# Attention decays of a hybrid GLA layer: prefix sums over tokens by a VectorE scan instead of 0/1 matrices on TensorE

## The chip, the cores and the metric

The kernel runs on one core of one Trainium2 chip. The metric is the device time of one execution in microseconds. The core's engines work beside each other, each through its own instruction queue in order: TensorE (PE; its weight loads are PEld), VectorE (DVE), ScalarE (ACT), GpSimd (POOL), and SyncE (SP), which here only issues DMA transfers. An instruction that waits for a semaphore holds everything behind it on its engine.

## The reference

One layer over 256 latent tokens (2048 channels) with 256 context tokens: a token mixer (gated linear attention beside a pooling mixer, merged by gates) and a SwiGLU feed-forward part. The change touches only the decays of the attention. Cut to that:

```python
q, k, v, g, a_lr, p, bg = jnp.split(proj, SPLIT_POINTS, axis=-1)
for d in range(2):                       # two directions
    z = a_lr[..., d*16:(d+1)*16] @ w_decay_up[d] + b_decay_up[d]
    log_decay.append(_heads(jax.nn.log_sigmoid(z) / 16.0, HEAD_K))

# per head, chunks of 64 tokens
cum = jnp.cumsum(log_a, axis=3)          # running sum over the tokens of a chunk
ref = cum[:, :, :, 31:32]
q_in, k_in = q * jnp.exp(cum - ref), k * jnp.exp(ref - cum)
scores = where(lower_triangle, q_in @ k_in.T, 0)
last = cum[:, :, :, -1:]
q_inter, k_state = q * jnp.exp(cum), k * jnp.exp(last - cum)
decay_chunk = jnp.exp(last)              # carries the state from chunk to chunk
```

There are 4 heads with 256 key channels and 512 value channels each. The context is scanned first, and its final state is where the latent tokens start.

The modulation, `silu(c) @ w_ada + b_ada`, yields six vectors of 2048 channels per condition. Only those for the first sub-layer's input are needed early; the others are needed behind the attention.

## The kernel before

All matrix products run on fp32 operands split into a high and a low part (fp32r). Weights arrive as units of 128x1024 numbers (512 KB): SP issues the transfer into a buffer `raw`, ScalarE writes `hi` (L100), VectorE subtracts to get `lo` (L101), and TensorE multiplies. `ws_tile` (L130, L134) has the weight stationary and yields channels by tokens; `nat_block` (L160, L161, L163) has the activations stationary and yields tokens by channels. The three buffers of each kind and eight PSUM banks set how far ahead this can run. A scheduler with priorities and a cost model sets each engine's order when the kernel is built; the splits have a raised priority.

The stages in time: modulation of the input and projection v (0 to 236 us), projection k for latent and context tokens with the low-rank decay rows `alr` (`kT_half`, 236 to 334), projection q of heads 0 and 1 (`qT_half(0)`, 334 to 356), the attention (356 to 606), which includes `front(0)`, the gate projection `g_block(0)`, `qT_half(1)`, and a loop over the heads of `back(h)`, `front(h+1)` and `g_block(h+1)`, then the pooling projection; then gates and merging (610 to 930), output projection and norm (to 1060), feed-forward in (to 1540) and out (to 1792).

`front(h)` makes, for each of two directions d, all decay factors of a head, multiplies q and k by them, and forms the masked score matrices PT (latent) and PC (context). `log_sigmoid` (L461 on) multiplies `alr` by the decay weights `wd` to get z with tokens on the partitions, and splits the log decay into `la` high and low. Sums over tokens are then matrix products with `cm`, a constant of 0/1 matrices (L507 for the context, L521 for the latent tokens), whose results ScalarE exponentiates straight from PSUM (L510, L522, L523) and VectorE multiplies by q or k (L511, L533 to L542). The score matmuls are L550, L553, L558 and L564. `back(h)` applies them to v.

The rest of the modulation is filler: `ada(n)` takes the next n units of `w_adaT`, for each of which SP moves 512 KB into a buffer `ra` and VectorE does one multiply with a sum (L269). `ADA` says how many are taken where: 4 per tile of projection k, 1 per tile of projection q, 8 per head, and 2 per step (16 steps, `ct`) of the gates stage, with what is left in its last steps. `ra` has three buffers during projection k and `qT_half(0)`, one in the attention, and two in the gates stage.

Of the kernel before, what the change touches and what calls it, by code (L numbers as in the profile page):

```python
# [41 lines left out]
ADA = (0, 1, 4, 2, 8, 8)  # L42
# [14 lines left out]
C_LAT = (0, 512)  # L57
C_CTX = 1024
C_N = 1664


@with_exitstack
def trunk(ctx, tc, small, consts, masks, xT, ctxT, x_nat, lnrows, wdec, pmat, c_row,
# [162 lines left out]
    with ExitStack() as c1:  # L226
# [156 lines left out]
        pk = c1.enter_context(sub_pool("pk"))  # L383
        cQ = ExitStack()
# [30 lines left out]
        def kT_half(b):  # L415
# [43 lines left out]
        def log_sigmoid(h, d, base, wd, ztmp):  # L459

            la = pg.tile([P, U], F32R, tag="la", bufs=2, name=nm("la")).rearrange("p (s t d) -> p s t d", s=2, t=2)  # L461
            z = bank("g")
            for t in range(2):
                PE.matmul(z[:, t * HK:(t + 1) * HK], alr[:, base + t * P:base + (t + 1) * P], wd[:, d, :],
                          start=(t == 0), stop=True, skip_group_check=True)
            e = ztmp
            S.activation(e, z, AF.Abs)
            S.activation(e, e, AF.Exp, scale=-1.0)
            S.activation(e, e, AF.Ln, bias=1.0)
            V.scalar_tensor_tensor(e, z, 0.0, e, op0=ALU.min, op1=ALU.subtract)  # L470
            split(e.rearrange("p (t d) -> p t d", t=2), la[:, 0], la[:, 1])
            return la

# [7 lines left out]
        def front(h):  # L481
            hb, ho = divmod(h, 2)
            wr = pg.tile([P, 2, HK], F32, tag="tmp", bufs=2, name=nm("wr"))
            nc.gpsimd.dma_start(wr, wdec[:, :, h * HK:(h + 1) * HK])
            wd = pg.tile([P, 2, HK], F32R, tag="wd", bufs=1, name=nm("wd"))
# [3 lines left out]
            kTh = kT[hb][:, 2 * ho:2 * ho + 2, :]  # L489
            qTh = qT[hb][:, 2 * ho:2 * ho + 2, :]  # L490
            kch = kTc[hb][:, 2 * ho:2 * ho + 2, :]
            PT = pg.tile([P, 4, P], F32, tag="PT", bufs=NPT, name=nm("PT"))
            PC = pg.tile([P, 2, T], F32, tag="PC", bufs=NPT, name=nm("PC"))
            for d in range(2):
                bun = hcp.tile([P, 4096], F32, tag="hc", name=nm("bun"))
                E = bun[:, :2304].rearrange("p (c n) -> p c n", c=2)
                kst = bun[:, 2304:2816].rearrange("p (c j) -> p c j", c=2)
                q4 = bun[:, 2816:3328].rearrange("p (c t i) -> p c t i", c=2, t=2)
                zt = bun[:, 3328:3840]

                la = log_sigmoid(h, d, T, wd, zt)
                ex = bank("g")
                for c in range(2):
                    for t in range(2):
                        b = C_CTX + 256 * d + 128 * (1 - t)
                        for s in range(2):
                            PE.matmul(ex[:, c * T:(c + 1) * T], la[:, s, t, c * P:(c + 1) * P], cm[:, b:b + T],  # L507
                                      start=(c == 0 and t == 0 and s == 0), stop=(t == 1 and s == 1),
                                      skip_group_check=True)
                S.activation(kst, ex.rearrange("p (c j) -> p c j", c=2), AF.Exp, scale=1.0 / 16.0)  # L510
                V.tensor_tensor(kst, kst, kch, op=ALU.mult)  # L511

# [562 lines left out]
```

## Time and profile before

| what | us |
|---|---|
| median of 3 runs | 1794.83 (1792.32 to 1798.92) |
| the profiled execution, its own time | 1794.45 |
| its span, first to last instruction | 1792.5 |
| TensorE busy in it | 1753.0 |
| mean granted clock of TensorE | 0.993 of full speed |

The profile is of one execution. A matmul's listed length runs past the start of the next one, since matmuls are pipelined; what one costs is the distance from its start to the start of the next. The same holds, to a lesser degree, for VectorE. A wait is listed at the engine that stood idle, with the instruction that ended it. Line numbers are those of the kernel before; in the changed kernel the same helpers stand five lines higher (L101 is L96 there, L130 is L125, L160 is L155, L269 is L264).

### The profile page before, as it was taken

To read this page: it belongs to the slowest core of one execution; us is meant where nothing else is said; L and a number is where in the kernel's file an instruction comes from. 1 tells how busy PE (TensorE), PEld (TensorE's weight loads), DVE (VectorE), ACT (ScalarE), POOL (GpSimd) and SP (SyncE) were. 2 spreads that over 40 slices of the span, in tenths; PEclk is the share of its full clock that TensorE was granted. 3 is DMA by queue.
4 is the path that set the end of the run, shared out by engine and by line. 5 is a ranking of instruction groups with operands and counts; after the bars stand their busy time and mean duration, and the time that the engine had idled before them with its cause. 6 is when DMAs were issued, how large, how long until landed. Compare 5 with 4: busy or idle time off the path is not lost.

```text
span 1792.5 us, 24735 instructions
## 1 busy us (share of the span) xinstructions
PE 1753.0 (98%) x9549; PEld 1468.0 (82%) x9551; DVE 1165.6 (65%) x1725; ACT 801.7 (45%) x1179; POOL 8.0 (0%) x17
## 2 busy tenths in 40 slices
PE   8999999999999999999999989999999999999996
PEld 5667878877777788888887878888888888888886
DVE  3665466576898576776666766666666666554555
ACT  2212222374776454444444464445444444443432
POOL 0000000000000000000000000000000000000000
PEclk9999999999999999999999999999999999999998
DMA  9895258755566467777786635577777766556553
GB/s 385 295 358 183 83 201 283 244 171 176 171 206 211 165 221 248 236 236 257 236 288 219 210 118 189 188 246 259 246 236 247 237 233 234 188 191 196 191 189 126
DMA packets 109350, 394.16 MB, mean 220 GB/s; under 512 B 12176, under 2 KB 12304, under 8 KB 108720
## 3 DMA queue, kind: packets, MB, share of 16 engines
q1 hardware_dynamic: 107712, 385.10, 63.0%
q0 software_dynamic: 1520, 7.47, 1.1%
q8 instruction: 75, 1.23, 0.3%
q14 instruction: 43, 0.35, 0.1%
HBM read 390.43 MB, written 2.10 MB: 219 GB/s over the span
## 4 chain that ended last, share of the span: by engine, by line
PE 75%; DVE 5%; DMA 3%; ACT 2%; issue 1%; SPq 0%; ACTq 0%; DVEq 0%
PE ps L130 33%; PE ps L134 17%; PE ps L160 6%; PE ps L161 6%; PE ps L163 6%; DMA raw<-in_w_o 1%; DVE lo L101 1%; ACT hi L100 1%; PE ps L564 1%; DMA ra<-in_w_adaT 1%; PE ps L592 1%; DVE ra L269 1%; PE ps L550 1%; PE ps L521 0%; PE ps L407 0%
## 5 line engine op out<-in xcount | busy, mean ns | idle before, releaser
L101 DVE TENSOR_TENSOR lo<-raw,hi 128x1024 fp32r<-128x1024 f32 x510 | 623.3, 1224 | 462.6 <-ACT hi L100 446.7
L100 ACT ACTIVATE hi<-raw 128x1024 fp32r<-128x1024 f32 x510 | 539.9, 1060 | 689.6 <-PE ps L130 263.8
L130 PE MATMUL ps<-h,hi 128*128 128x512 f32 x1408 | 353.4, 392 | 0.8 <-DVE h L101 0.8
L130 PEld LDWEIGHTS ps<-h,hi 128*128 128x128 f32 x1408 | 253.3, 189 | 46.5 <-DVE h L101 1.2
L130 PE MATMUL ps<-hl,hi 128*128 128x512 f32 x768 | 211.9, 393 | 0.0
L134 PEld LDWEIGHTS ps<-h,lo 128*128 128x128 f32 x1408 | 192.5, 190 | 13.9
L134 PE MATMUL ps<-h,lo 128*128 128x256 f32 x1408 | 196.8, 282 | 0.0
L130 PEld LDWEIGHTS ps<-hl,hi 128*128 128x128 f32 x768 | 139.8, 189 | 25.3
L160 PE MATMUL ps<-hi,hid 128*128 128x512 f32 (+1 forms) x372 | 134.9, 369 | 0.0
L161 PE MATMUL ps<-hi,hid 128*128 128x512 f32 (+1 forms) x372 | 134.0, 369 | 0.0
L160 PE MATMUL ps<-hi,hl 128*128 128x512 f32 x320 | 128.0, 400 | 2.0 <-ACT hi L100 2.0
L161 PE MATMUL ps<-hi,hl 128*128 128x512 f32 x320 | 125.6, 393 | 0.0
L134 PE MATMUL ps<-hl,lo 128*128 128x256 f32 x768 | 120.7, 282 | 0.0
L269 DVE SCALAR_TENSOR_TENSOR ra<-ra,silb 128x1024 f32<-128x1024 f32 x96 | 114.9, 1221 | 8.6 <-DMA ra<-in_w_adaT 7.9
L134 PEld LDWEIGHTS ps<-hl,lo 128*128 128x128 f32 x768 | 111.8, 190 | 6.8
L163 PE MATMUL ps<-lo,hl 128*128 128x512 f32 x320 | 92.7, 391 | 0.0
L163 PE MATMUL ps<-lo,hid 128*128 128x512 f32 x372 | 90.6, 369 | 0.0
L347 DVE TENSOR_TENSOR v<-ps,v 128x512 f32<-128x512 f32 x80 | 50.5, 684 | 55.6 <-PE ps L163 55.5
L160 PEld LDWEIGHTS ps<-hi,hid 128*128 128x128 f32 x372 | 69.8, 188 | 12.2 <-DVE xt L776 0.2
L161 PEld LDWEIGHTS ps<-hi,hid 128*128 128x128 f32 x372 | 70.0, 188 | 11.8
L160 PEld LDWEIGHTS ps<-hi,hl 128*128 128x128 f32 x320 | 60.0, 188 | 21.6 <-issue 5.2
L163 PEld LDWEIGHTS ps<-lo,hid 128*128 128x128 f32 x372 | 66.2, 188 | 11.8
(250 smaller groups left out, 2096.6 us busy)
## 6 DMA issues: line engine op xcount, KB each, us to landing
raw<-in_w_fi SPq DMA_DIRECT2D x176, 512.0 KB, 4.2
ra<-in_w_adaT SPq DMA_DIRECT2D x96, 512.0 KB, 4.6
raw<-in_w_fo SPq DMA_DIRECT2D x88, 512.0 KB, 4.3
rw<-in_w_sh_sc SPq DMA_DIRECT2D x64, 512.0 KB, 7.1
raw<-in_w_bg SPq DMA_DIRECT2D x64, 512.0 KB, 4.3
raw<-in_w_v SPq DMA_DIRECT2D x32, 512.0 KB, 5.1
raw<-in_w_g SPq DMA_DIRECT2D x32, 512.0 KB, 3.9
raw<-in_w_go SPq DMA_DIRECT2D x32, 512.0 KB, 3.4
```

Source lines behind the costliest of these rows:

```text
L100: S.activation(hi, full, AF.Copy)
L101: last_split[:] = [V.tensor_tensor(lo, full, hi.bitcast(F32), op=ALU.subtract)]
L130: PE.matmul(o, hi[:, j * P:(j + 1) * P], act(n + j), start=(n + j == 0), stop=(n + j == nk - 1), skip_group_check=True)
L134: PE.matmul(o[:, :T], lo[:, j * P:(j + 1) * P], act(n + j)[:, :T], start=False, stop=(n + j == nk - 1), skip_group_check=True)
L160: PE.matmul(o, ah, hi[:, a:b], start=(n + j == k0), stop=False)
L161: PE.matmul(o, al, hi[:, a:b], start=False, stop=False)
L163: PE.matmul(o, ah, lo[:, a:b], start=False, stop=(n + j == end))
L269: V.scalar_tensor_tensor(r, r, 1.0, silb[half], op0=ALU.mult, op1=ALU.mult, accum_out=mods[:, half, i:i + 1])
L347: V.tensor_tensor(dst, src, dst, op=ALU.add)
L550: PE.matmul(sc[:, t * P:(t + 1) * P], E[:, c, b + (512 if b == 0 else 384):b + (640 if b == 0 else 512)], E[:, c, b:b + 128], start=first, ...
L564: PE.matmul(scc[:, t * T:(t + 1) * T], kst[:, c, t * P:(t + 1) * P], q4[:, c].rearrange("p t i -> p (t i)"), start=(c == 0 and t == 0), st ...
L592: PE.matmul(os[t], PC[:, j, t * P:(t + 1) * P], vc[h][:, j, :], start=(j == 0), stop=False)
```

## The change

The 0/1 matrices, `log_sigmoid` with its split, and the products L507 and L521 go. z is now made with `wd` stationary, 128 channels by all 512 tokens (context and latent) per matmul, 4 per head (two channel halves by two directions). For each direction one `tensor_tensor_scan` on VectorE over 128 partitions by 1024 (two channel halves by 512 tokens) yields the running sums; a mask that is 0 at the segments' starts resets them. Sums over other ranges come by subtraction (VectorE), then ScalarE's exponentials run from SBUF to SBUF, then VectorE multiplies by k, and behind a `yield` by q.

`decay_up(h)`, which loads and prepares `wd`, is apart from `front` and has a pool of its own. `front(0)` is started before `qT_half(0)` and its two steps stand around it, so that the pool of projection k with its three `ra` buffers is closed before `qT_half(0)`. ADA becomes 2 per tile of q, 4 per tile of k but for the first, 3 per step of the gates stage, and 2 per head.

```diff
-ADA = (0, 1, 4, 2, 8, 8)
+ADA = (0, 2, 4, 3, 8, 2)
...
                 if b == 0 and i == 0:
                     decay_rows()
-                ada(ADA[2])
+                else:
+                    ada(ADA[2])
...
+        def front(h, wd):
...
             for d in range(2):
...
+                x = xs[d]
                 for c in range(2):
...
+                    z = bank("g")
+                    PE.matmul(z, wd[:, d, c * P:(c + 1) * P], alr, start=True, stop=True)
+                    e = x[:, d + 512 * c:d + 512 * c + 512]
+                    S.activation(e, z, AF.Abs)
+                    S.activation(e, e, AF.Exp, scale=-1.0)
+                    S.activation(e, e, AF.Ln, bias=1.0)
+                    V.scalar_tensor_tensor(e, z, 0.0, e, op0=ALU.min, op1=ALU.subtract)
...
+                if d == 0:
+                    V.tensor_tensor_scan(Wf, mask, x[:, 0:1024], 0.0, op0=ALU.mult, op1=ALU.add)
+                else:
+                    V.tensor_tensor_scan(Wf, x[:, 0:1024], mask, 0.0, op0=ALU.add, op1=ALU.mult)
...
+                V.tensor_tensor(G.rearrange("p c (n i) -> p c n i", n=4), W64,
+                                W64[:, :, :, 31 + d:32 + d].to_broadcast([P, 2, 4, 64]), op=ALU.subtract)
+                V.tensor_tensor(TT.rearrange("p c t n i -> p c t (n i)"), Wl,
+                                Wl[:, :, :, 63 + d:64 + d].to_broadcast([P, 2, 2, P]), op=ALU.subtract)
...
+                S.activation(ep, G, AF.Exp, scale=sc16)
+                S.activation(G, G, AF.Exp, scale=-sc16)
...
+                V.tensor_tensor(k1, k1, kh, op=ALU.mult)
+                V.tensor_tensor(TT[:, :, :, d, :], TT[:, :, :, d, :], kv[:, :, :, d, :], op=ALU.mult)
+                V.tensor_tensor(k3, k3, kh[:, :, f * P:(f + 1) * P], op=ALU.mult)
+                V.tensor_tensor(kst, kst, kch, op=ALU.mult)
+                yield
...
+                V.tensor_tensor(q1, q1, qh, op=ALU.mult)
...
-        qT_half(0)
         cQ.close()
...
-        st_ = run(front(0))
+        f0 = front(0, decay_up(0))
+        next(f0)
+        qT_half(0)
+        next(f0)
+        next(f0)
         gs = [g_block(0)]
+        st_ = run(f0)
         qT_half(1)
...
-            ada(ADA[3] if ct < 14 else 128)
+            ada(ADA[3] if ct < 15 else 128)
```

The order of the instructions at the places that matter, first TensorE in `front(0)`, direction 0. `hi` and `lo` are weight units, `cm` and `la` the 0/1 matrices and the log decay, `bun` the bundle of decay factors. Before, sums over the latent tokens stand among the units of `g_block(0)`:

```order
L160 MATMUL ps468_3044<-hi482_3119,hl1_78 128x512
L161 MATMUL ps468_3044<-hi482_3119,hl1_78 128x512
L521 MATMUL ps447_2897<-cm_2849,la445_2887 128x512 [waits Activation_49]
L521 MATMUL ps448_2902<-cm_2849,la445_2887 128x384 [waits PE_49]
L521 MATMUL ps449_2907<-cm_2849,la445_2887 128x512 [waits PE_49]
L521 MATMUL ps450_2912<-cm_2849,la445_2887 128x384 [waits DVE_49]
L160 MATMUL ps467_3043<-hi482_3119,hl1_78 128x512
L161 MATMUL ps467_3043<-hi482_3119,hl1_78 128x512
L521 MATMUL ps447_2897<-cm_2849,la445_2887 128x512 [waits DVE_49]
```

After, the score matmuls (L559, L562, L566) follow projection q's last unit directly, with one matmul of `g_block(0)` between the first three:

```order
L125 MATMUL ps433_2842<-hl1_78,hi438_2867 128x512 x7
L129 MATMUL ps433_2842<-hl1_78,lo439_2868 128x256 [waits DVE_49]
L129 MATMUL ps433_2842<-hl1_78,lo439_2868 128x256 x7
L559 MATMUL ps442_2900<-bun403_2654 128x128 [waits DVE_49]
L559 MATMUL ps442_2900<-bun403_2654 128x128
L155 MATMUL ps448_2951<-hi451_2955,hl0_77 128x512 [waits Activation_49]
L562 MATMUL ps442_2900<-bun403_2654 128x128 [waits DVE_49]
L566 MATMUL ps442_2900<-bun403_2654 64x64 x2
L559 MATMUL ps442_2900<-bun403_2654 128x128 x2
L562 MATMUL ps442_2900<-bun403_2654 128x128
L566 MATMUL ps442_2900<-bun403_2654 64x64 x2
```

L521 (four matmuls here, the fifth, and three more behind it) is gone, and the waits for VectorE of the scores' first parts (L559, L562) have a single other matmul between them.

Next VectorE at the same place; `ra` is a modulation unit, `lo` a weight split. Before, the multiplications by q and k of direction 0 run in one piece, with one split inside and no modulation unit near:

```order
L526 COPY tot451_2917<-bun441_2865 128x2 [waits Activation_49]
L533 TENSOR_TENSOR bun441_2865<-bun441_2865,qT_2644 128x2x128
L534 TENSOR_TENSOR bun441_2865<-bun441_2865,kT_1827 128x2x128
L540 TENSOR_TENSOR bun441_2865<-bun441_2865,qT_2644 128x2x128
L540 TENSOR_TENSOR bun441_2865<-bun441_2865,kT_1827 128x2x128 [waits Activation_49]
L540 TENSOR_TENSOR bun441_2865<-bun441_2865,qT_2644 128x2x64
L540 TENSOR_TENSOR bun441_2865<-bun441_2865,kT_1827 128x2x64
L101 TENSOR_TENSOR lo492_3174<-raw490_3171,hi491_3173 128x1024 [waits DMAHW5_49,PE_49,Activation_49]
L536 TENSOR_TENSOR bun441_2865<-bun441_2865,qT_2644 128x2x128
L540 TENSOR_TENSOR bun441_2865<-bun441_2865,qT_2644 128x2x128
L540 TENSOR_TENSOR bun441_2865<-bun441_2865,kT_1827 128x2x128
```

After, from behind the last split of projection q's weights to the multiplication (L550 of the changed kernel) that the score matmul L562 waits for:

```order
L139 SCALAR_TENSOR_TENSOR qT_2682<-ps406_2683,qT_2682 128x256
L139 SCALAR_TENSOR_TENSOR qT_2682<-ps415_2736,qT_2682 128x256 [waits Activation_49]
L264 SCALAR_TENSOR_TENSOR ra422_2783,mods_75<-ra422_2783,silb321_2050 128x1024 [waits DMAHW3_49]
L96 TENSOR_TENSOR lo452_2956<-raw450_2953,hi451_2955 128x1024 [waits DMAHW6_49,PE_49,Activation_49]
L139 SCALAR_TENSOR_TENSOR qT_2682<-ps424_2789,qT_2682 128x256 [waits Activation_49]
L547 TENSOR_TENSOR bun403_2654<-bun403_2654,qT_2682 128x512 [waits DVE_49]
L548 TENSOR_TENSOR bun403_2654<-bun403_2654,qT_2682 128x4x64
L96 TENSOR_TENSOR lo455_2974<-raw453_2971,hi454_2973 128x1024 [waits DMAHW7_49,PE_49,Activation_49]
L264 SCALAR_TENSOR_TENSOR ra423_2786,mods_75<-ra423_2786,silb321_2050 128x1024 [waits DMAHW1_49,DVE_49]
L549 TENSOR_TENSOR bun403_2654<-bun403_2654,qT_2682 128x2x128
L550 TENSOR_TENSOR bun403_2654<-bun403_2654,qT_2682 128x2x128
```

Two modulation units (ra422, ra423), which share one buffer now, and two splits stand among the multiplications by q (L547 to L550).

Last VectorE where projection v ends and projection k begins; `v3` is the last block of v as it leaves PSUM. Before:

```order
L269 SCALAR_TENSOR_TENSOR ra315_1974,mods_75<-ra315_1974,silb313_1965 128x1024 [waits DVE_49]
L269 SCALAR_TENSOR_TENSOR ra316_1977,mods_75<-ra316_1977,silb313_1965 128x1024
L101 TENSOR_TENSOR lo310_1872<-raw308_1869,hi309_1871 128x1024 [waits DMAHW3_49,PE_49,Activation_49]
L269 SCALAR_TENSOR_TENSOR ra317_1980,mods_75<-ra317_1980,silb313_1965 128x1024
L269 SCALAR_TENSOR_TENSOR ra318_1983,mods_75<-ra318_1983,silb313_1965 128x1024 [waits DMAHW6_49,DVE_49]
L101 TENSOR_TENSOR lo323_1991<-raw321_1988,hi322_1990 128x1024 [waits DMAHW4_49,PE_49,Activation_49]
L347 TENSOR_TENSOR v3_411<-ps293_1748,v3_411 128x512
L347 TENSOR_TENSOR v3_411<-ps294_1749,v3_411 128x512
L347 TENSOR_TENSOR v3_411<-ps295_1750,v3_411 128x512
L347 TENSOR_TENSOR v3_411<-ps296_1751,v3_411 128x512
```

And after:

```order
L342 TENSOR_TENSOR v2_360<-ps285_1682,v2_360 128x512
L342 TENSOR_TENSOR v2_360<-ps286_1683,v2_360 128x512
L96 TENSOR_TENSOR lo310_1875<-raw308_1872,hi309_1874 128x1024 [waits DMAHW3_49,PE_49,Activation_49]
L178 SCALAR_TENSOR_TENSOR raw322_2052<-silb321_2050,raw322_2052 128x1024 [waits DVE_49,Activation_49]
L96 TENSOR_TENSOR lo317_1973<-raw315_1970,hi316_1972 128x1024 [waits DMAHW4_49,PE_49,Activation_49]
L342 TENSOR_TENSOR v3_411<-ps293_1748,v3_411 128x512
L342 TENSOR_TENSOR v3_411<-ps294_1749,v3_411 128x512
L342 TENSOR_TENSOR v3_411<-ps295_1750,v3_411 128x512
L342 TENSOR_TENSOR v3_411<-ps296_1751,v3_411 128x512
L180 TENSOR_TENSOR silb321_2050<-silb321_2050,raw322_2052 128x1024 [waits Activation_49]
L96 TENSOR_TENSOR lo320_2011<-raw318_2008,hi319_2010 128x1024 [waits DMAHW5_49,PE_49,Activation_49]
L264 SCALAR_TENSOR_TENSOR ra323_2059,mods_75<-ra323_2059,silb321_2050 128x1024 [waits DVE_49]
```

The four modulation units that stood ahead of v3 (ra315 to ra318) are gone from there, and the first now comes behind it (ra323); a piece of the silu of the condition (raw322) has come between the splits.

## Rows read from the trace of the kernel before

**Rows 1.** Page, part 1: busy time of each engine, share of the span, instructions.

```profile
PE 1753.0 (98%) x9549; PEld 1468.0 (82%) x9551; DVE 1165.6 (65%) x1725; ACT 801.7 (45%) x1179; POOL 8.0 (0%) x17
```

**Rows 2.** Stretches: from, to, length, then busy us (instructions) per engine, clock, DMA share.

```profile
334.20:606.00 271.80, 266.42 (x1296) 208.84 (x1295) 212.81 (x398) 168.18 (x311) 3.24 (x5) 1.00 0.56 189
620.00:915.00 295.00, 295.00 (x1705) 260.19 (x1704) 206.10 (x285) 146.01 (x217) 0.00 (x0) 1.00 0.71 237
236.30:239.70 3.40, 3.38 (x8) 2.71 (x9) 0.56 (x1) 0.00 (x0) 0.00 (x0) 0.50 0.70 270
```

**Rows 3.** TensorE's timeline: start, length, line, operation; the 0/1-matrix products and their successors.

```profile
365.93 0.99 PE L507 MATMUL ps<-cm,la 128*128 128x256 f32 x7
366.76 0.63 PE L163 MATMUL ps<-lo,hl 128*128 128x512 f32 x2
...
370.89 1.08 PE L521 MATMUL ps<-cm,la 128*128 128x512 f32 x4
371.81 0.39 PE L160 MATMUL ps<-hi,hl 128*128 128x512 f32 x1
...
395.97 1.79 PE L521 MATMUL ps<-cm,la 128*128 128x512 f32 x8
397.59 0.40 PE L130 MATMUL ps<-hl,hi 128*128 128x512 f32 x1
```

**Rows 4.** TensorE's timeline: two projection units, then one direction's score matmuls.

```profile
348.05 2.00 PE L130 MATMUL ps<-hl,hi 128*128 128x512 f32 x8
...
350.85 2.00 PE L130 MATMUL ps<-hl,hi 128*128 128x512 f32 x8
...
378.82 0.45 PE L550 MATMUL ps<-bun 128*128 128x128 f32 x2
...
382.68 0.59 PE L464 MATMUL ps<-wd,alr 128*128 128x256 f32 x2
```

**Rows 5.** Waits of TensorE, 334 to 606 us: total us, times, longest.

```profile
PE ps L550 <- DVE bun L540: 2.3, 3, 1.5
PE ps L521 <- ACT la L100: 1.0, 1, 1.0
PE ps L507 <- ACT la L100: 0.9, 1, 0.9
```

**Rows 6.** VectorE's timeline: successive instructions of 512, 256 and 1024 elements per partition.

```profile
368.63 0.69 DVE L511 TENSOR_TENSOR bun<-bun,kTc 128x512 f32<-128x512 f32 x1
369.23 0.69 DVE L470 SCALAR_TENSOR_TENSOR bun<-ps,bun 128x512 f32<-128x512 f32 x1
...
375.37 0.42 DVE L540 TENSOR_TENSOR bun<-bun,qT 128x256 f32<-128x256 f32 x1
375.70 0.42 DVE L540 TENSOR_TENSOR bun<-bun,kT 128x256 f32<-128x256 f32 x1
...
376.44 1.22 DVE L101 TENSOR_TENSOR lo<-raw,hi 128x1024 fp32r<-128x1024 f32 x1
377.57 0.42 DVE L536 TENSOR_TENSOR bun<-bun,qT 128x256 f32<-128x256 f32 x1
```

**Rows 7.** TensorE's timeline where projection v ends and projection k begins.

```profile
232.33 0.39 PE L130 MATMUL ps<-hl,hi 128*128 128x512 f32 x1
236.32 0.79 PE L130 MATMUL ps<-hc,hi 128*128 128x512 f32 x1 [3.60 <-DVE v L347]
...
237.34 0.63 PE L130 MATMUL ps<-hc,hi 128*128 128x512 f32 x1
237.76 0.63 PE L130 MATMUL ps<-hl,hi 128*128 128x512 f32 x1
```

**Rows 8.** VectorE's timeline over the same place; the bracket is idle time before.

```profile
232.09 1.23 DVE L269 SCALAR_TENSOR_TENSOR ra<-ra,silb 128x1024 f32<-128x1024 f32 x1 [0.96 <-DMA ra<-in_w_adaT]
...
233.24 1.22 DVE L101 TENSOR_TENSOR lo<-raw,hi 128x1024 fp32r<-128x1024 f32 x1
234.38 2.48 DVE L347 TENSOR_TENSOR v<-ps,v 128x512 f32<-128x512 f32 x4
```

**Rows 9.** Waits of VectorE for modulation weights, 236 to 620 us.

```profile
DVE ra L269 <- DMA ra<-in_w_adaT: 6.2, 5, 3.4
```

**Rows 10.** Page, part 6: issues of the modulation weights, median us to landing.

```profile
ra<-in_w_adaT SPq DMA_DIRECT2D x96, 512.0 KB, 4.6
```

More of the change, by code (lines that the diff above doesn't have):

```diff
@@ L383, in trunk @@
         pk = c1.enter_context(sub_pool("pk"))
+        cW = ExitStack()
+        pw = cW.enter_context(sub_pool("pw"))
         cQ = ExitStack()
@@ L457, in trunk @@
         og = {}
[L459 to L472, printed above, removed]
         def run(gen):
@@ L479, in run, with decay_up @@
                     return e.value
-        def front(h):
-            hb, ho = divmod(h, 2)
-            wr = pg.tile([P, 2, HK], F32, tag="tmp", bufs=2, name=nm("wr"))
+        def decay_up(h):
+            wr = pw.tile([P, 2, HK], F32, tag="wr", name=nm("wr"))
             nc.gpsimd.dma_start(wr, wdec[:, :, h * HK:(h + 1) * HK])
-            wd = pg.tile([P, 2, HK], F32R, tag="wd", bufs=1, name=nm("wd"))
+            wd = pw.tile([P, 2, HK], F32R, tag="wd", bufs=2, name=nm("wd"))
             S.activation(wd, wr, AF.Copy)
@@ L494, in front @@
             for d in range(2):
[L495 to L509, printed above, removed]
@@ L541, in front @@
-                for c in range(2):
-                    V.tensor_scalar(q4[:, c, s_, :], E[:, c, 768:896], tot[:, c:c + 1], None, op0=ALU.mult)
+                bun = hcp.tile([P, 4096], F32, tag="hc", name=nm("bun"))
+                Wf = bun[:, 0:1024]
+                W = Wf.rearrange("p (c s) -> p c s", c=2)
+                Wl = W[:, :, 0:T].rearrange("p c (t i) -> p c t i", t=2)
+                G = bun[:, 1024:1536].rearrange("p (c s) -> p c s", c=2)
+                ep = bun[:, 1536:2048].rearrange("p (c s) -> p c s", c=2)
@@ L625, in trunk @@
         ada_bufs.append(1)
-        cm = pg.tile([P, C_N], F32R, tag="cm", name="cm")
         mk = pg.tile([P, 2, P], I32, tag="mk", name="mk")
         nc.gpsimd.dma_start(mk.rearrange("p a b -> p (a b)"), masks)
-        for a, b in ((0, U), (U, C_N)):
-            r = wp.tile([P, U], F32, tag="raw", name=nm("raw"))
-            nc.sync.dma_start(r[:, :b - a], consts[:, a:b])
-            S.activation(cm[:, a:b], r[:, :b - a], AF.Copy)
-        st_ = run(front(0))
+        mask = pg.tile([P, U], F32, tag="mask", name="mask")
+        nc.gpsimd.memset(mask, 1.0)
+        nc.gpsimd.memset(mask.rearrange("p (c s i) -> p c s i", c=2, s=4)[:, :, 0:3, 0:1], 0.0)
+        xs = [pg.tile([P, U + 2], F32, tag=f"x{d}", name=f"x{d}") for d in range(2)]
+        nc.gpsimd.memset(xs[1][:, 0:1], 0.0)
+        f0 = front(0, decay_up(0))
[3 more added lines that the diff above has]
+        next(f0)
         gs = [g_block(0)]
+        st_ = run(f0)
         qT_half(1)
         for h in range(H):
-            f = front(h + 1) if h + 1 < H else None
+            f = front(h + 1, decay_up(h + 1)) if h + 1 < H else None
             if f:
@@ L647, in trunk @@
         cG.close()
+        cW.close()
         py = c1.enter_context(sub_pool("py"))
@@ L1027, in _layout @@
         "small": small,
-        "consts": _decay_consts(np),
         "masks": _score_masks(np),
```

108 lines of the change are left out of this document (47 added, 61 removed).

## The prediction

> **What bounds the kernel now.** I read first the engines' busy shares: TensorE is busy for 1753.0 us of the 1792.5 us span, VectorE for 1165.6 us [rows 1]. The reader is to see that at this level only TensorE's own work and its few gaps can set the time. Then I cut the span at the stages that the change touches. From the end of projection k to the end of the heads (334.2 to 606.0 us) TensorE is busy for 266.42 of 271.80 us, and VectorE for 212.81, which is 78% [rows 2]. In the gates stage TensorE has no gap at all in 295.00 us, VectorE is at 206.10, and DMA at 0.71 [rows 2]. Third, TensorE's own timeline, for what each removed matmul occupies [rows 3, 4]. Fourth, the list of TensorE's waits in the attention: 2.3 us for the multiplications ahead of the scores, 1.0 and 0.9 us for the high part of the log decay [rows 5]. Last, the place where projection k begins, the longest wait near the change: 3.60 us for v, and then a slower spell [rows 7].
>
> So an edit gains by taking TensorE's work away, and loses by making its queue wait for VectorE. This change does both.
>
> **What the matrices cost.** Seven L507 matmuls occupy 366.76 - 365.93 = 0.83 us, 0.119 each [rows 3]. There are 64: 7.6 us. Four L521 matmuls occupy 371.81 - 370.89 = 0.92 us, eight elsewhere 397.59 - 395.97 = 1.62 us [rows 3]; the 64 (8 per direction and head) cost 8 x 1.62 = 13.0 to 8 x 1.84 = 14.7, and I take 13.7. z costs the same either way: half as many matmuls, twice as wide. The score matmuls keep their number. Term one: **-21.3 us** of TensorE's work, nearly all of it in a stage where TensorE is busy for 98%.
>
> **Its gaps of before.** The stage has 271.80 - 266.42 = 5.4 us of idle time [rows 2]. The two waits for the log decay's high part, 1.9 us [rows 5], lose their instructions. The 2.3 us ahead of the scores will be other waits in the new order. I take out all, **-5.4 us**, and count what is late next afresh below.
>
> **Where projection k begins.** VectorE stood 0.96 us for a modulation unit, worked on it, then on a split, and only at 234.38 began to take v out of PSUM [rows 8]. TensorE's third bank came free at 236.32 [rows 7]. [...] The new order has no modulation unit ahead of v3. But lo317 and a silu step are still there, and the three evacuations that the bank needs take 3 x 0.60 us [rows 6] from the last v matmul at about 232.3. So at least some 2 us of the wait stay. Bounds: 0 and -3.2 (wait down by 1.6, slow spell gone, eight matmuls by 0.2 each). I take **-1 us**, nearer to nothing, since VectorE is in one piece busy there before and after.
>
> **What VectorE gets.** Occupied time, start to start: 512 elements 0.60 us, 256 elements 0.33, 1024 elements 1.13 [rows 6]; 128 elements I put at 0.2. Removed per head and direction: two splits of `la` 1.2, L511 0.6, seven multiplications of 256 elements 2.3, six of 128 1.2: 5.3 us. Added: differences G and TT 1.2, the others 0.8 as a mean over the directions, k's four multiplications 1.9, q's five 1.9, and the scan. The trace has no scan. It reads two inputs of 1024 elements, so I bound it by one pass of such a row, 1.13 us, and two, 2.26 us: each element needs a multiplication and an addition that wait for the element before. Nothing lies below one pass, since no two-input row of fp32 is faster. I take two passes. That gives 8.1 us, +2.8 per head and direction, +22 in eight. By the low bound it is +13.
>
> [...]
>
> Against that, modulation units leave: 32 were taken in q's tiles and the heads (4 + 4 + 24), now 22 (8 + 8 + 6): -10 x 1.13 = -11 us. VectorE goes from 212.81 to about 224 us (215 by the low bound), while TensorE's span shrinks to some 250: 86 to 90% instead of 78%. ScalarE loses the 16 splits and stays far below (168.18 us [rows 2]).
>
> This load is uneven. From projection k's end to `qT_half(1)`'s end, TensorE has 24 units at 2.80 us (two 16-matmul halves of a tile start 350.85 - 348.05 apart) and two score groups of about 3.9 [rows 4]: 75 us. VectorE's new order has there 24 splits and 12 modulation units, 41 us, two scans 4.5, twenty-two rows of 512 13, twenty-seven of 256 9: 68 us, 90%. Over the rest of the heads, without the pooling projection, the same count gives 125 us against some 134 of TensorE.
>
> **The waits that come.** In `front(0)`, direction 0, ra423 may be fetched only once ra422 has been used, since one buffer is left, and it lands 4.6 us after its issue [rows 10]. The score matmul L562 needs two multiplications of 256 behind it: 4.6 + 1.13 + 0.67 = 6.4 us after ra422's end. L559 needs only a split, a fold, and two multiplications: 1.13 + 0.33 + 0.60 + 0.33 = 2.4 us after it. Between L559 and L562 TensorE has 0.4 us of work. So L562 waits for 6.4 - 2.4 - 0.4 = 3.6 us if L559 comes just in time, and less if it comes late; I take 3. What stands behind it is `g_block(0)`, ready but held. Direction 1 has four modulation units in a chain ahead of its scores, but the eight units of `g_block(0)`, 22 us, stand beside them: 2 us. The six direction passes of the heads have two modulation units per head in the same buffer: between 0.3 us each, what rows 5 give as a mean over eight, and 3 us, the price of the first. I take 1 us, nearer to the row: 6 us. Term four: **+11 us**, bounds +2 and +24.
>
> **The gates stage** gets 46 units instead of 32, 14 x 1.13 = +16 us of VectorE in 295 us (206 to 222, 75%) and 7 MB more DMA on SP's queue. TensorE has no gap there, and a unit waits for nobody but the next. I cost it at nothing; if the weight splits came late behind a modulation wait, the longest such wait is 3.4 us [rows 9]. The end of this stage has the same two units ahead of the output projection's weights on SP as before. `decay_up` and the mask's fill on GpSimd have other work beside them: nothing.
>
> **Sum.** 1794.45 - 21.3 - 5.4 - 1 + 11 = 1777.8 us for the profiled execution, which lies 0.4 us below the median of 1794.83; so 1778 us.
>
> **Rivals.**
> - *All waits hidden.* Splits are made up to three buffers ahead, so the queue may ride through. The waits stay at 2.3 us as before: 1794.8 - 27.7 + 2.3 = 1769 us. For it: VectorE waited for modulation units only 5 times, 6.2 us in all, with one buffer [rows 9]. Against it: its load rises by some ten points.
> - *VectorE takes TensorE's place in the heads.* Scores wait in every pass, and the freed matmul time becomes idle time, so that the change does not do what it says. At the upper bound, +24 us: 1794.8 - 27.7 + 24 = 1791 us. For it: 125 us against 134 with a chain of matmul, three ScalarE steps, scan, differences, exponentials and products in each pass. Against it: this chain may run a head ahead.
> - *Slower: the single `ra` buffer.* The twelve units in q's tiles come two per tile of 5.6 us, with a landing of 4.6 us and 1.13 us of use each, so they cannot keep that pace; VectorE's queue, weight splits included, would go at theirs. If each holds VectorE for the longest wait seen, 3.4 us [rows 9], that is 12 x 3.4 = 41 us, and with the heads' 6 us 1794.8 - 27.7 + 47 = 1814 us. It decides from 27.7 / 12 = 2.3 us per unit uncovered. Against it: VectorE has other work between most units, and SP issues the next right behind the use.
>
> **How the numbers follow.** About 0.5% (9 us) is what a measurement of this kernel can tell from no change: below 1786 is faster, above 1804 slower. Forecast 0.45 (its own range 1772 to 1785), all hidden 0.20, VectorE the bound 0.25, slower 0.10. Faster: 0.45 + 0.20, plus a third of the third case, 0.07: 0.72. Slower: the last, of which some would end within: 0.08. The rest, 0.20, is the same. The range takes in the second and third case with the bounds of the waits, and leaves the last: 1765 to 1796.
>
> **What would show it.** Right: no gap over 4 us in the attention, the stage from projection k's end to the heads' end some 255 to 262 us long against 271.8, a scan near 2.3 us, and TensorE's longest new wait at L562 in `front(0)`. Wrong on the first term: TensorE's busy time falls by much less than 21 us. Wrong on the waits: more than 20 us of waits of the score matmuls for VectorE, or weight splits that wait behind L264. Wrong on the gates stage: any gap in it. If the wait at projection k's start is still 3.6 us, that term was nothing.

## The result, and the profile after

The changed kernel takes 1778.05 us (median of 4 runs, 1774.43 to 1781.06) against 1794.0 (4 runs, 1792.32 to 1798.92): a ratio of 0.9906, 95% interval 0.9879 to 0.9933. The forecast was 1778. The profiled execution took 1777.96 us with a span of 1776.1 us, 16.5 us less than that of before.

The page's first part, to be held against [rows 1], shows TensorE down by 20.1 us and VectorE up by 15.8:

```profile
PE 1732.9 (98%) x9407; PEld 1452.2 (82%) x9407; DVE 1181.4 (67%) x1701; ACT 791.8 (45%) x1137; POOL 9.1 (1%) x20
```

To find where the time went, both spans are cut at the same three events: the last tile of projection k leaves PSUM, the last part of the pooling projection leaves PSUM, and the last split of the merged rows (`mT`) starts, at the end of the gates stage. The stretch between the first two is called the attention here (it takes in projection q of heads 0 and 1), that between the last two the gates stage. Of the kernel before (from, to, length, busy us of PE, PEld, DVE, ACT and POOL, clock, DMA share, GB/s):

```profile
335.50:609.90 274.40, 269.02 (x1307) 211.03 (x1306) 213.05 (x399) 169.28 (x311) 3.24 (x5) 1.00 0.56 190
609.90:944.30 334.40, 334.40 (x1912) 294.43 (x1912) 232.09 (x330) 164.64 (x247) 1.05 (x2) 1.00 0.71 239
```

And of the kernel after, with a third row for a short stretch inside the attention:

```profile
334.80:591.60 256.80, 246.75 (x1164) 194.33 (x1163) 216.16 (x352) 157.61 (x266) 1.81 (x3) 0.99 0.53 182
591.60:925.50 333.90, 333.90 (x1910) 294.10 (x1909) 246.06 (x350) 164.63 (x248) 1.05 (x2) 1.00 0.76 262
433.40:437.00 3.60, 3.57 (x13) 3.19 (x14) 2.81 (x7) 0.00 (x0) 0.00 (x0) 0.53 0.84 311
```

The attention went from 274.40 to 256.80 us, 17.6 us less. TensorE's busy time there fell by 22.3 us, and its gaps (the time of the stretch in which it is not busy) rose from 5.4 to 10.05 us. The gates stage took 14 more units and 14 us more of VectorE in the same time, TensorE without a gap in either kernel. Ahead of the attention the changed kernel is 0.7 us quicker, and behind the gates stage, where nothing was forecast, 2.4 us slower (850.6 against 848.2 us); no run tells why. The third row is looked at in the last section.

TensorE's waits between 336 and 592 us in the kernel after, which answer to [rows 5] (total us, times, longest):

```profile
PE ps L559 <- DVE bun L547: 4.8, 4, 1.8
PE ps L614 <- DVE o L612: 2.9, 2, 1.9
PE ps L562 <- DVE bun L550: 1.9, 1, 1.9
PE ps L614 <- DVE st L185: 0.4, 1, 0.4
```

All ten microseconds are waits for VectorE: 6.7 us ahead of the scores (L559, L562), and 3.3 us in `back` (L614), which before had 0.2. TensorE's timeline, at four places (in brackets its idle time before the instruction, and what ended it):

```profile
355.23 1.11 PE L129 MATMUL ps<-hl,lo 128*128 128x256 f32 x8
356.18 0.61 PE L559 MATMUL ps<-bun 128*128 128x128 f32 x4
...
358.88 0.49 PE L562 MATMUL ps<-bun 128*128 128x128 f32 x2 [1.86 <-DVE bun L550]
...
387.42 0.68 PE L559 MATMUL ps<-bun 128*128 128x128 f32 x4 [1.82 <-DVE bun L547]
...
433.43 1.00 PE L614 MATMUL ps<-sm,o 128*128 128x128 f32 x4 [1.91 <-DVE o L612]
...
235.57 0.78 PE L125 MATMUL ps<-hc,hi 128*128 128x512 f32 x1 [3.17 <-DVE v L342]
```

The third row shown, L562, waits 1.86 us in `front(0)`, direction 0; L559 waits 1.82 us in direction 1. Behind L562 on TensorE stands L156 of `g_block(0)`, on the weight unit that L155 had used at 356.55 us; it starts at 360.92. VectorE's timeline shows what L562 waited for:

```profile
351.05 1.22 DVE L264 SCALAR_TENSOR_TENSOR ra<-ra,silb 128x1024 f32<-128x1024 f32 x1
...
354.60 1.22 DVE L96 TENSOR_TENSOR lo<-raw,hi 128x1024 fp32r<-128x1024 f32 x1
356.92 1.23 DVE L264 SCALAR_TENSOR_TENSOR ra<-ra,silb 128x1024 f32<-128x1024 f32 x1 [1.11 <-DMA ra<-in_w_adaT]
...
358.07 0.42 DVE L549 TENSOR_TENSOR bun<-bun,qT 128x256 f32<-128x256 f32 x1
358.41 0.42 DVE L550 TENSOR_TENSOR bun<-bun,qT 128x256 f32<-128x256 f32 x1
```

The unit of L264 at 351.05 is ra422. The next, ra423, begins at 356.92, after 1.11 us of idle time for its transfer, some 4.7 us behind ra422's end; and the two multiplications of 256 (L549, L550) that L562 needs come after it. That is the chain through the single buffer `ra`.

The scans, both directions (duration in ns, least, median and most):

```profile
L506 DVE TENSOR_TENSOR_SCAN bun<-mask,x x4: 2290/2292/2292, 339.6 to 512.8; 128x1024 f32<-128x1024 f32 x4
...
L508 DVE TENSOR_TENSOR_SCAN bun<-x,mask x4: 2283/2284/2286, 374.8 to 536.4; 128x1024 f32<-128x1024 f32 x4
```

### The profile page after: what moved, and what is told of

The parts are those of the page before. It is cut to its first block, busy times and chain, and to the rows that moved or that the text cites. A ratio compares the mean times of both kernels' runs of the same rounds, so it can differ in the third digit from the quotient of the medians.

```text
span 1776.1 us, 24344 instructions
## 1 busy us (share of the span) xinstructions
PE 1732.9 (98%) x9407; PEld 1452.2 (82%) x9407; DVE 1181.4 (67%) x1701; ACT 791.8 (45%) x1137; POOL 9.1 (1%) x20
## 4 chain that ended last, share of the span: by engine, by line
PE 74%; DVE 7%; DMA 3%; ACT 1%; issue 1%; DVEq 0%; ACTq 0%
PE ps L125 33%; PE ps L129 17%; PE ps L158 6%; PE ps L156 6%; PE ps L155 6%; DVE lo L96 2%; DMA ra<-in_w_adaT 1%; DMA raw<-in_w_o 1%; PE ps L572 1%; DMA raw<-in_w_fi 1%; ACT hi L95 1%; PE ps L559 1%; PE ps L599 0%; DVE bun L508 0%; DVE ra L264 0%
## 5 line engine op out<-in xcount | busy, mean ns | idle before, releaser
L96 DVE TENSOR_TENSOR lo<-raw,hi 128x1024 fp32r<-128x1024 f32 x510 | 623.1, 1223 | 436.8 <-ACT hi L95 425.0
L155 PE MATMUL ps<-hi,hid 128*128 128x512 f32 (+1 forms) x372 | 134.9, 369 | 0.0
L156 PE MATMUL ps<-hi,hid 128*128 128x512 f32 (+1 forms) x372 | 134.0, 369 | 0.0
L155 PE MATMUL ps<-hi,hl 128*128 128x512 f32 x320 | 128.2, 401 | 1.4 <-ACT hi L95 1.4
L156 PE MATMUL ps<-hi,hl 128*128 128x512 f32 x320 | 125.8, 394 | 0.0
L264 DVE SCALAR_TENSOR_TENSOR ra<-ra,silb 128x1024 f32<-128x1024 f32 x96 | 115.0, 1221 | 15.5 <-DMA ra<-in_w_adaT 15.5
L155 PEld LDWEIGHTS ps<-hi,hid 128*128 128x128 f32 x372 | 69.9, 188 | 12.2 <-DVE xt L788 0.2
L156 PEld LDWEIGHTS ps<-hi,hid 128*128 128x128 f32 x372 | 69.9, 188 | 11.9
L155 PEld LDWEIGHTS ps<-hi,hl 128*128 128x128 f32 x320 | 60.3, 189 | 21.2 <-issue 5.4
```

The lines of the kernel that those rows point to most:

```text
L96: last_split[:] = [V.tensor_tensor(lo, full, hi.bitcast(F32), op=ALU.subtract)]
L155: PE.matmul(o, ah, hi[:, a:b], start=(n + j == k0), stop=False)
L156: PE.matmul(o, al, hi[:, a:b], start=False, stop=False)
L264: V.scalar_tensor_tensor(r, r, 1.0, silb[half], op0=ALU.mult, op1=ALU.mult, accum_out=mods[:, half, i:i + 1])
```

## The experiments

Each was timed in 5 rounds beside the kernel before. The last three columns, in us, are of the one profiled execution of each, over the attention as cut above. The sum over tokens is left out in e3 (in part), e4, e6 and e9. The order of the instructions is made anew for each kernel; only e4 has that of the kernel it is compared with.

```
                        median   ratio to before (95%)    attention us   TensorE busy   VectorE busy
before                  1794.8                             274.4          269.0          213.1
after                   1778.05  0.9906 (0.9879-0.9933)    256.8          246.8          216.2
e1  units as before     1783.15  0.9932 (0.9918-0.9945)    265.2          251.2          226.8
e2  units alone         1792.80  0.9983 (0.9974-0.9991)    273.4          268.8          201.4
e3  half the matrices   1795.98  1.0007 (0.9998-1.0015)    273.6          261.1          212.2
e4  one pass, no scan   1769.69  0.9858 (0.9843-0.9873)    248.8          245.1          208.4
e5  matmuls added       1794.79  0.9999 (0.9990-1.0007)    277.3          269.0          217.7
e6  removal alone       1787.32  0.9964 (0.9951-0.9976)    264.6          252.5          202.9
e7  no units            1802.05  1.0048 (1.0035-1.0061)    250.7          245.1          191.5
e8  front(0) late       1778.08  0.9910 (0.9896-0.9923)    254.4          246.0          215.0
e9  removal and units   1782.47  0.9924 (0.9910-0.9939)    259.6          249.1          191.0
e10 units earlier       1777.24  0.9899 (0.9886-0.9912)    255.0          246.8          207.3
e11 e10 and bias        1775.74  0.9887 (0.9872-0.9902)    252.5          246.2          203.1
e12 load off the chain  1782.43  0.9921 (0.9906-0.9935)    262.2          249.1          225.1
```

**e1, the scan with the units where they were.**

```diff
-ADA = (0, 2, 4, 3, 8, 2)
+ADA = (0, 1, 4, 2, 8, 8)
```

> The changed kernel with the modulation units taken where the kernel before takes them (per tile of q 1 instead of 2, per head 8 instead of 2, per gates step 2 instead of 3, and 4 also in the first tile of k). The scan stays. Theory (the gain is TensorE's removed matmuls less waits for VectorE, and the moves only ease VectorE): VectorE gets 10 units, 11 us, back between projection k's end and the heads' end; L562's wait of 1.9 us in front(0) goes with the shorter chain of units, the waits of the heads grow by 3 to 10 us: 1780 to 1787 us, so at least half of the 16 us gain stays. Rival (the moved units carry the gain): back to 1790 us or above.

Measured 1783.15 us: the theory's range. About 11 of the 16 us come without the moves. In the attention VectorE is busy 10.7 us longer, and TensorE has 14.0 us of gaps. More than half of them is one wait, 7.1 us for a head's scores, and the clock over the attention is 0.98:

```profile
PE ps L558 <- DVE bun L546: 9.5, 3, 7.1
PE ps L613 <- DVE o L611: 3.4, 3, 2.2
```

**e2, the units alone.** The kernel before with the edit of e1 the other way round.

> The kernel before, with 0/1 matrices, with only the modulation units moved as in the changed kernel. Theory: before, TensorE's waits in the attention were 4.4 us in all, and only those 2.3 us ahead of the scores could shrink; with the wait at projection k's start shorter by half a microsecond: 1790 to 1795 us, no difference that can be told. Rival (the moved units carry the gain): 1783 us or below.

Measured 1792.80 us, 2 us faster, as the theory had it: with the matrices there, VectorE has 11.7 us less to do in the attention, and the attention is only 1.0 us shorter by it. Alone the parts give 11.6 and 2 us; together 16.

**e3, half the matrices.**

```diff
-                        for s in range(2):
-                            PE.matmul(ex[:, :n], la[:, s, t, c * P:(c + 1) * P], cw[:, :n], start=(s == 0), stop=(s == 1))
+                        PE.matmul(ex[:, :n], la[:, 0, t, c * P:(c + 1) * P], cw[:, :n], start=True, stop=True)
```

(and likewise for L507.)

> The kernel before without the products of the low part of the log decay: 32 of the 64 L507 and 32 of the 64 L521 matmuls are left out, and nothing else. By their slots, 32 x 0.119 and half of 13.7, that is 10.7 us of TensorE's work. Theory (a removed matmul is worth its slot): 1782 to 1785 us. Rival (they ran while TensorE would have waited for splits or for VectorE anyway): above 1789 us.

Measured 1795.98 us, no gain at all: the theory fell. The attention, and TensorE's waits in it:

```profile
335.40:609.00 273.60, 261.12 (x1243) 202.98 (x1242) 212.16 (x399) 170.11 (x311) 3.25 (x5) 0.99 0.59 190
```

```profile
PE ps L520 <- ACT la L100: 6.1, 3, 4.1
PE ps L160 <- ACT hi L100: 1.6, 1, 1.6
PE ps L163 <- DVE lo L101: 1.5, 2, 0.7
```

TensorE's busy time fell by 7.9 us, its gaps rose from 5.4 to 12.5 us. The largest wait is for the high part of `la`, once for 4.1 us: a link of the chain from z to the scores, which the matmuls had lain beside. The order of the other instructions is new here, so the run shows that the freed time became waits, but not that no other order would have used it.

**e4, the scan at the price of one pass.** All other instructions keep their order, on every engine, so this is the cleanest of the runs.

```diff
-                    V.tensor_tensor_scan(Wf, mask, x[:, 0:1024], 0.0, op0=ALU.mult, op1=ALU.add)
+                    V.tensor_tensor(Wf, mask, x[:, 0:1024], op=ALU.max)
```

> The changed kernel with each of the eight scans (2.29 us in the trace) replaced by one two-input pass over the same tiles (a maximum, 1.13 us), which leaves the running sums out; every other instruction and the order stay. VectorE has 8 x 1.15 = 9.2 us less work in the stage where TensorE waits for it for 10 us. Theory (these waits come from VectorE's load ahead of the scores): L559's 4.8 us shrink by 2 to 4 us, 1773 to 1776 us. Rival (the waits come from the order and the single buffer of the modulation units, not from the scan): same time within 1 us, 1777 to 1779 us.

Measured 1769.69 us, 8.4 us less than the changed kernel, beyond what the theory said and against the rival. A two-input pass of 1024 elements is listed at 1.22 us in the changed kernel (L96) against the scan's 2.29, so by an estimate VectorE has 8 x 1.07 = 8.6 us less to do (not 9.2, as expected; its busy time in the attention fell by 7.8), and this came through almost one for one. The attention and TensorE's waits in it:

```profile
334.40:583.20 248.80, 245.13 (x1163) 192.72 (x1162) 208.35 (x351) 156.95 (x266) 1.82 (x3) 1.00 0.57 187
```

```profile
PE ps L559 <- DVE bun L547: 1.5, 1, 1.5
PE ps L614 <- DVE o L612: 1.2, 1, 1.2
PE ps L562 <- DVE bun L550: 0.7, 1, 0.7
```

Gaps 3.7 us instead of 10.05, and the clock at 1.00 instead of 0.99.

**e5, the matmuls put back as idle work.**

```diff
+                du = bank("g")
+                for n in (256,) * 8 + (512,) * 4 + (384,) * 4:
+                    PE.matmul(du[:, :n], wd[:, d, 0:P], alr[:, :n], start=True, stop=True)
```

> The changed kernel with 16 matmuls added per head and direction (eight of 256, four of 512 and four of 384 columns, the shapes of L507 and L521) on operands that are there early, into a bank that nobody reads; by their slots 8 x (8 x 0.119 + 4 x 0.23 + 4 x 0.18) = 21 us of TensorE's work that waits for nothing. Theory (TensorE's work sets the time, its waits for VectorE are only the 10 us of its gaps): these matmuls fill at most those 10 us, so +11 to +21 us: 1789 to 1799 us. Rival (since half the matrices out of the kernel before gained nothing, the attention is set by the chain and VectorE, and the matmuls are hidden): below 1784 us.

Measured 1794.79 us, 16.7 us more, in the theory's range; the whole gain is gone.

```profile
332.10:609.40 277.30, 269.02 (x1289) 213.78 (x1288) 217.73 (x352) 158.51 (x266) 1.82 (x3) 0.99 0.51 168
```

The attention is 20.5 us longer, with 22.3 us more of TensorE's work and gaps of 8.3 us instead of 10.05: in the changed kernel nearly all of the work shows. (The profiled execution was 2.7 us quicker to the end of projection k. The added matmuls also hold a PSUM bank; what that costs is not measured apart.)

**e6, the removal alone.** In the kernel before `log_sigmoid` returns its result `e` without the split, L507 and L521 go, and the exponentials read `e`:

```diff
-            split(e.rearrange("p (t d) -> p t d", t=2), la[:, 0], la[:, 1])
-            return la
+            return e
...
-                        ex = bank("g")
-                        for s in range(2):
-                            PE.matmul(ex[:, :n], la[:, s, t, c * P:(c + 1) * P], cw[:, :n], start=(s == 0), stop=(s == 1))
+                        ex = la
```

> The kernel before with all the L507 and L521 matmuls and the 16 splits of la left out and nothing put in their place: the exponentials read the log decays' first matmul (z) in PSUM, so the sums over tokens are missing. TensorE loses 21.3 us, VectorE 9.7, ScalarE 9.9, and the chain from z to the scores loses two links. Theory (the matmuls count once the chain through la is gone too; e3 took matmuls and left the chain): 1767 to 1772 us. Rival (the attention before was not TensorE's to give, something else holds it): above 1780 us.

(The expectation is wrong in one point: what the exponentials read is not z in PSUM but the log decay `e` in SBUF, one tile of which serves the context and then the latent tokens.)

Measured 1787.32 us, 7.5 us less: the rival's side. With all of the matrices and splits gone and nothing in their place, the kernel is slower than with the scan, also than e1, which has the units at the same places (1783.15 us). The attention, and VectorE's waits for units in it, which answer to [rows 9]:

```profile
335.70:600.30 264.60, 252.53 (x1179) 196.47 (x1178) 202.87 (x384) 163.74 (x295) 3.24 (x5) 0.98 0.60 197
```

```profile
DVE ra L269 <- DMA ra<-in_w_adaT: 14.8, 11, 4.3
```

There are 12 us of gaps and a clock of 0.98, so that TensorE's busy time falls by 16.5 us and not by 21.3. VectorE stands 14.8 us for the units' single buffer, where before it was 6.2.

**e7, no units in the attention.**

```diff
-ADA = (0, 2, 4, 3, 8, 2)
+ADA = (0, 0, 4, 4, 8, 0)
...
-            ada(ADA[3] if ct < 15 else 128)
+            ada(ADA[3] + (ct > 11) if ct < 15 else 128)
```

> The changed kernel with no modulation unit between projection k's end and the heads' end: 28 in projection k as now, 68 in the gates stage (4 per step, 5 in steps 12 to 14, 5 in the last). VectorE loses 22 x 1.13 = 25 us in the attention, and the single buffer has no user. Theory (from e4: about 0.9 us per us of VectorE's load, until TensorE's 10 us of waits are used up): waits fall to 2 or 3 us, 1769 to 1772 us, if the gates stage hides its 22 added units as it did the 14. Rival (gates stage at 206 + 41 = 247 of 295 us of VectorE and a two-buffer queue behind a landing of 4.6 us now waits): 1775 us or above, with gaps in the gates stage.

Measured 1802.05 us: the theory was wrong on the gates stage, where the rival was right. In the attention (250.7 us) 6.1 us came off, as it had it, though 5.6 us of gaps stay where it said 2 or 3. Attention and gates stage:

```profile
335.00:585.70 250.70, 245.07 (x1163) 192.51 (x1162) 191.45 (x308) 153.82 (x262) 1.82 (x3) 1.00 0.44 142
585.70:942.70 357.00, 340.45 (x1902) 295.99 (x1901) 266.25 (x388) 172.61 (x254) 1.05 (x2) 0.98 0.78 269
```

In the attention 24.7 us less of VectorE's work made it 6.1 us shorter, a quarter of a microsecond for each, where e4 had nearly one. The gates stage is 23 us longer than after, with 16.6 us of gaps and a clock of 0.98. TensorE waits in it for the high parts of weights, which ScalarE could not make because their transfers were late. SP issues these transfers and the units' in one queue, and VectorE waited 21.7 us in 23 places for units to land (9.1 us in 15 places in the changed kernel). TensorE's waits, then ScalarE's longest:

```profile
PE ps L125 <- ACT hi L95: 11.8, 8, 6.7
PE ps L155 <- ACT hi L95: 2.4, 2, 1.4
```

```profile
ACT hi L95 <- DMA raw<-in_w_bg: 68.5, 32, 4.3
```

So, counted from the kernel before, 14 more units there cost nothing, and 36 more cost 23 us. Another 6.8 us are lost behind the gates stage (857.4 against 850.6 us).

**e8, front(0) behind the whole of `qT_half(0)`.**

```diff
+        qT_half(0)
         cQ.close()
...
-        next(f0)
-        qT_half(0)
-        next(f0)
-        next(f0)
+        st_ = run(f0)
         gs = [g_block(0)]
-        st_ = run(f0)
```

> The changed kernel with front(0) whole behind qT_half(0), as in the kernel before, whose units then have projection k's three buffers. Theory (L562's 1.9 us wait is the one-buffer chain of ra422 and ra423 among the multiplications by q): that wait goes; but the chain z, scan, exponentials of front(0) then stands beside g_block(0) alone, and scores at its end wait as much: 1776 to 1781 us. Rival (starting front(0) early is what hides the chain): 1783 us or above, with a wait of over 5 us in front(0).

Measured 1778.08 us, the same as the changed kernel. L562's 1.9 us wait for VectorE is gone, and L559 waits 5.1 us in five places. Starting `front(0)` early, with the single buffer for the units of projection q that comes with it, is worth nothing here; the run moves both, so it does not show the worth of either alone.

**e9, e6 with the units moved** (the edit of e2 on top).

> The kernel of e6 (0/1 matrices and splits of la left out, sums over tokens missing) with the modulation units taken as in the changed kernel. In e6 VectorE waited 14.8 us for modulation units in the attention, against 6.2 before, and TensorE stood 12 us. Theory (with TensorE's work gone, 24 units through one buffer at some 5.7 us each are the next limit in the heads, and the moved units are what lets the removal count): 1770 to 1776 us, 11 to 17 below e6, where the same move was worth 2 us to the kernel before (e2). Rival (e6 is held by something else, such as the bank of z that the exponentials keep): above 1781 us.

Measured 1782.47 us, with runs from 1776.27 (the profiled one) to 1784.37: 4.8 us below e6, not the 11 to 17 expected. The units, by their work or by their buffer (the run changes both), were a part of what held e6, but not most of it. The attention, and TensorE's largest wait in it:

```profile
333.80:593.40 259.60, 249.08 (x1179) 194.09 (x1178) 191.03 (x361) 162.94 (x295) 3.24 (x5) 0.99 0.55 179
```

```profile
PE ps L540 <- DVE bun L530: 6.2, 5, 2.6
```

Gaps are 10.5 us with the least VectorE load of all kernels, and 6.2 of them are again the scores' waits for VectorE's multiplications. What makes these late is left open; the version differs from the changed kernel in making z twice per pass, once for the context and once for the latent tokens, in keeping the tile of the log decay through all the exponentials, and in more and smaller instructions.

**e10, units earlier.**

```diff
-ADA = (0, 2, 4, 3, 8, 2)
+ADA = (0, 1, 5, 3, 8, 2)
```

> The changed kernel with 5 units instead of 4 per tile of projection k and 1 instead of 2 per tile of q: 35 in k (VectorE is there at 59.8 of 93.0 us, TensorE without a gap), 8 in q, 6 in the heads, 47 in the gates stage. VectorE loses 8 x 1.13 = 9 us between projection k's end and qT_half(1)'s end. Theory (e4's 0.9 us per us, but only on the waits that stand there, L562's 1.9 and L559's 1.8 us in front(0)): 1773 to 1776 us. Rival (waits move on to the next scores, as the heads are VectorE's): 1777 to 1779 us, the same as the changed kernel.

Measured 1777.24 us, the rival's number. 9 us of VectorE less in the attention made it 1.8 us shorter. The scores' waits fell from 6.7 to 2.3 us, but in the new order a wait came that the changed kernel does not have, for the high part of a weight in the heads:

```profile
PE ps L155 <- ACT hi L95: 3.3, 1, 3.3
```

So the 1.8 us are net of this wait, and not the worth of the moved units alone.

**e11, e10 with three differences per head as a bias column of ScalarE's exponential.**

```diff
-                    V.tensor_tensor(eq, tot.to_broadcast([P, 2, 2, P]), Wl, op=ALU.subtract)
+                    V.tensor_scalar(tot, tot, 1.0 / 16.0, None, op0=ALU.mult)
...
+                            S.activation(eq[:, c, t, :], Wl[:, c, t, :], AF.Exp, scale=-sc16, bias=tot[:, c, t, :])
```

> The kernel of e10 with three differences per head (for the chunk and context sums) made by ScalarE, as a bias column of its exponential, instead of by VectorE: 256 + 512 + 512 elements, 1.5 us per head less on VectorE, 0.2 us of scaling more; ScalarE gets 3 instructions more per direction and head, some 0.6 us each pass. Theory (VectorE ahead of the scores sets the heads' waits): 4 x 1.3 = 5 us of VectorE times 0.9, another -3 to -5 us against e10: 1769 to 1773 us. Rival (ScalarE's longer chain to the exponentials takes its place, or the weight splits wait for ScalarE): no better than e10.

Measured 1775.74 us, 1.5 us below e10: less than the theory's 3 to 5 us, and the intervals of the two overlap. It is the fastest version that computes the reference, though its interval overlaps that of the changed kernel as well.

**e12, load behind the scores' operands.**

```diff
                 evac(PT[:, 2 + d, :], sc[:, 256:384], 1)
+                V.tensor_tensor(x[:, d:d + 1024], x[:, d:d + 1024], mask, op=ALU.mult)
```

> The changed kernel with one pass of 1024 elements (1.13 us, on a tile that nobody reads again) added per head and direction on VectorE, behind the multiplications that feed the scores: 8 x 1.13 = 9 us of VectorE, the mirror of e4's 9.2 us, but off the way from z over the scan to the scores. Theory as it stands after e10 and e11 (9 and 5 us of VectorE's load taken away elsewhere gained 1 and 1.5 us, so what counts is the length of the chain in front of the scores, not the load): 1778 to 1782 us. Rival (VectorE's load counts wherever it stands): 1784 to 1788 us.

Measured 1782.43 us, between the two. In the attention:

```profile
335.10:597.30 262.20, 249.09 (x1163) 195.56 (x1162) 225.07 (x359) 157.15 (x266) 1.81 (x3) 0.99 0.54 178
```

It is 5.4 us longer for 9 us of VectorE off the chain, where e4 took 8.0 us off for 8.6 us on it. That speaks for both, place and load, but does not settle how much each counts: e4 kept the order of the instructions and e12 did not, and e12's runs (1777.12 to 1783.79 us) overlap those of the changed kernel.

## Why the prediction was right

- **The matrices, -21.3 us: right in size** (busy time of the same stage -22.3 us), and e5 shows that in the changed kernel this work is worth nearly its slots. But the sentence under it, that an edit gains by taking TensorE's work away, is not true by itself. e3 took 10.7 us of slots (7.9 us of busy time) and gained nothing, e6 took 21.3 (16.5) and gained 7.5. The changed kernel gained 11 us before its units were moved (e1) and 16 with them. What in it made the freed time count is not shown: its way from z to the scores no longer passes through a split and a second set of matmuls, but neither does e6's. The sum added up terms that don't add.
- **The gaps: right in sum.** 5.4 us were to go and 11 to come; 10.05 are there. By parts: L562 in `front(0)` 1.9 us where 3 were forecast, by the forecast mechanism to the instruction; direction 1 there 1.8 where 2 were; the other scores 3.0 where 6 were. 3.3 us in `back` (L614) were not foreseen: its normalised output stands in the same VectorE queue. The longest new wait is therefore not L562's, as forecast, but one of L614, 1.91 against 1.86 us.
- **The scan: right.** Two passes of a row were taken, 2.26 us; it is 2.29 as listed, and 2.2 from its start to the next start, which is how the passes were counted. The same trace has a single pass of such a row, the split L96, at 1.22 us. What the prediction undersold is the place: e4 shows that the second half of the scan alone costs the kernel 8.4 us. VectorE's load came out lower than summed up, 216.2 us in the attention where about 224 were forecast; as the scan has its price, the excess lies in the other rows of that count.
- **Projection k's start, -1 us: too much.** TensorE's wait is 3.17 us instead of 3.60, and the slower spell stayed: a clock of 0.52 where it was 0.50 [rows 2], and most matmuls 0.42 to 0.43 us apart in it, 0.22 to 0.24 behind it, in both kernels. That difference is the 0.2 us for each of eight matmuls in the term's bounds. With no unit ahead, v still leaves PSUM late, for the silu step and lo317 stand ahead of it:

```profile
231.36 1.23 DVE L178 SCALAR_TENSOR_TENSOR raw<-silb,raw 128x1024 f32<-128x1024 f32 x1 [3.31 <-ACT raw L177]
232.50 1.22 DVE L96 TENSOR_TENSOR lo<-raw,hi 128x1024 fp32r<-128x1024 f32 x1
233.64 2.48 DVE L342 TENSOR_TENSOR v<-ps,v 128x512 f32<-128x512 f32 x4
```

- **The gates stage, nothing: right** (333.9 against 334.4 us, with 14 us more of VectorE), and e7 shows where that ends.
- **The rivals.** All waits hidden did not happen: 10 us stayed, and only a cheaper scan (e4) came to 1769. VectorE as the bound is half true: a microsecond of its load counted for 0.2 (e10) to 0.9 (e4), but at 10 us of gaps TensorE is still the bound. The single buffer as a brake on everything did not happen with 22 units; with 32 (e6) VectorE waited 14.8 us for it, but no run shows what that alone cost.
- **The sum: luck in part.** It met the profiled execution to 0.2 us. The matrices gave 1.0 us more than forecast, the gaps came out 0.9 us smaller than the sum had them, and the 2.4 us lost behind the gates stage, which it left at nothing, made up for that. The stretch that the prediction named as its sign, projection k's end to the heads' end, is some 254 us long (its 271.8 less the 17.6 that the attention lost), just under its 255 to 262.

## What to carry to other kernels

A matmul taken from a TensorE that is busy for 98% need not be worth its slot (e3): find the chain that lay beside it, see whether the same edit takes links out of that as well, and then measure, since a chain with those two links gone was not enough either (e6). A cost on an engine has a place: a microsecond in front of what TensorE waits for was worth nearly itself (e4), the same microsecond elsewhere from a fifth (e10) and a quarter (e7) to six tenths (e12), each by the profiled execution, and the last three with a new order of the instructions. Filler work was free up to some number of units (14 more) and cost much beyond it (36 more), when the stage's transfers came late, so move it in steps and look for the first gap.

## What was not expected of the hardware

A wait of TensorE of 1.91 us, at 433.43 us in the changed kernel, was followed by a granted clock of 0.53 for 3.6 us (the third row of the stretches above): 0.66 up to 434.0 us, 0.50 from there to 437.0, and 1.00 in the microsecond behind. The waits of 1.86 and 1.82 us, at 358.88 and 387.42 us, were followed by a clock of 1.00, and the one of 3.17 us, at 235.57, by one of 0.52:

```profile
358.80:362.00 3.20, 3.12 (x21) 2.60 (x22) 2.81 (x8) 0.04 (x1) 0.00 (x0) 1.00 0.67 250
387.40:391.00 3.60, 3.58 (x24) 3.07 (x24) 3.60 (x7) 3.26 (x6) 0.00 (x0) 1.00 0.60 221
235.50:238.90 3.40, 3.33 (x8) 2.68 (x9) 1.75 (x3) 0.00 (x0) 0.00 (x0) 0.52 0.41 145
```

So waits of nearly the same length can differ in what they cost, here by some 1.7 us (an estimate: 3.6 us at 0.53 of the clock lose 0.47 x 3.6). Nor does the longest wait alone tell the clock of a stage: in the attention it is 0.98 in e1, where the longest wait is 7.1 us, and in e6, where it is 3.6 us, but 0.99 in e3 and e5, where it is 4.1 us.
